# Dilated attention with score terms as half-row matmuls of two heads, q and k recopied per branch, and fewer value loads

## The chip, the cores and the metric

One Trainium2 chip, one core. The time is the device time of one execution of the whole program in microseconds, as the median of several runs. Engines: PE (TensorE), DVE (VectorE), ACT (ScalarE), POOL (GpSimd) and SP (SyncE, which here only issues DMAs).

## What is computed

One step of a hybrid layer for a prompt of 2048 tokens and a few sample tokens: projections to q, k and v, a state-space scan (SSD), a dilated attention of 8 heads of 64, and behind them the trunk (gating, output projection, cross-attention, MLP). The change is in the attention of the prompt. Its three branches have (window, dilation) = (128, 1), (512, 4), (2048, 16); each has blocks of n = 128 queries of one residue, which see the keys of their own block and of the block before:

```python
def dilated_branch_prompt(q, k, v, window, dil):
    n = window // dil
    ...
    qb = to_blocks(q)
    kb = with_prev(to_blocks(k))
    vb = with_prev(to_blocks(v))
    s = jnp.einsum('brjqhd,brjkhd->brjhqk', qb, kb) * (HEAD_DIM ** -0.5)
    ...
    dist = a + n - c
    band = (dist >= 0) & (dist <= n)
    ...
    p, lse = softmax_stats(s)
    o = jnp.einsum('brjhqk,brjkhd->brjqhd', p, vb)
    ...
def combine_branches(outs, lses):
    w = jax.nn.softmax(jnp.stack(lses, axis=0), axis=0)
    return jnp.sum(w[..., None] * jnp.stack(outs, axis=0), axis=0)
```

## The kernel before, in words

The program runs phase_a (projections, 0 to about 300 us), phase_ssd (to about 670), phase_att (about 660 to 1057) and then the trunk. q and k are kept in DRAM as two parts each, a high and a low one (s_qh, s_ql, s_kh, s_kl), since a product in the fast form of fp32 would lose bits: a score is qh·kh + qh·kl + ql·kh. In DRAM the heads lie in 4 groups of two heads, 128 rows (2 x 64) by 2048 tokens.

phase_att works in 96 steps: 4 groups g, 3 branches b, 8 steps each; a step is 2 blocks of 128 queries for both heads (u = 0, 1). In step i the engines get, in this order: front(i), the scores on PE; soft(i), DVE's masked minimum (L995) and ACT's exponential (L997); back(i-2), the values of the step before the last (L1018), after every second step with a copy of the output to SBUF by ACT (L1028); flip(i-1), the transposes of the probabilities (L1005) with their copy to SBUF by DVE (L1010), one in four by ACT (L1008); then the actions that `at` has put down for this step. The first two steps run beside the end of phase_ssd.

The scores of one block (lines 976 to 987): per head one full-row matmul (L983) over 128 rows, where q stands twice, [qh; qh], and k as [kh; kl], and one half-row matmul (L986) over 64 rows for ql·kh. All are 256 keys wide. The keys lie in DRAM permuted within 128 tokens (lines 258 to 269), so that the views of branches 1 and 2 find runs of 8 keys; queries are read with a stride of 4 in branch 1 and of 16 in branch 2.

`load_qk` (lines 923 to 942) loads a group's q and k with 9 DMAs issued by GpSimd into 5 tiles of 1 MB; group g+1 is loaded at step 24g+1, into the other half of a double set of tiles. `load_v` (lines 944 to 959) loads the values with SP: 16 DMAs of 64 KB for branch 0 (L949), 16 for branch 1 (L954), one for branch 2 (L957); the first is called ahead of step 0.

The combine of group g starts at step 24g+24, and its parts follow at +0 (gather, L1053 to L1065: the statistics go to DRAM and come back as t_R), +5 (least, L1069 to L1072), +6 (exponentials, L1075, with products on GpSimd), +7 (coefficients, L1084 to L1094: to DRAM and back as t_cf), and then the products of outputs and coefficients on GpSimd (L1103, L1106), four chunks of 128x512 for three branches. It works in place in the output tiles t_o, of which there are 5. The last group's combine uses DVE too. Step 12 loads columns of gains for the trunk (trunk.weights; DVE scales one, g_gx, at L1435). The trunk's first residual tiles are loaded at steps 73 to 77 and the last three of eight after the last scores, by GpSimd (L1387).

Of the kernel before, what the change touches and what calls it, by code (L numbers as in the profile page):

```python
# [10 lines left out]
F32 = mybir.dt.float32  # L11
# [7 lines left out]
P = 128  # L19
# [8 lines left out]
def host_constants():  # L28
# [10 lines left out]
    off1 = (blk - 1) * P + 16 * (w % 8) + w // 8  # L39
    off2 = (blk - 1) * P + 32 * (w // 32) + 4 * (w % 8) + (w // 8) % 4  # L40
    m1 = np.where((a - off1 >= 0) & (a - off1 <= P), 0.0, BIG)
    m2 = np.where((a - off2 >= 0) & (a - off2 <= P), 0.0, BIG)
# [51 lines left out]
def weight_parts(nc, hi, lo, raw, g):  # L94
    """hi + lo = raw * g exactly to float32."""
    nc.scalar.activation(hi, raw, AF.Copy, scale=g)
    nc.vector.scalar_tensor_tensor(lo, raw, g, hi.bitcast(F32), op0=ALU.mult, op1=ALU.subtract)


def phase_a(E, arena, ssd):  # L100
    """q, k, v, dt of every token; x transposed, in two parts."""
    nc, tc = E.nc, E.tc
    with ExitStack() as ctx, ExitStack() as inner:
# [66 lines left out]
        def memory(j):  # L170
            """The memory's rows, transposed and scaled, in two parts."""
# [33 lines left out]
        def turn(i, b):  # L205
            """Rotary positions; the parts of a block of q | k | v | dt."""
# [29 lines left out]
        def finish(i):  # L236
# [11 lines left out]
            else:  # L248
# [3 lines left out]
                for o, dhi, dlo in ((0, E.s_qh, E.s_ql), (512, E.s_kh, E.s_kl)):  # L252
# [5 lines left out]
                    if o == 0:  # L258
                        nc.scalar.activation(hi, pq, AF.Copy)
                        nc.vector.tensor_tensor(lo, pq, hi.bitcast(F32), op=ALU.subtract)  # L260
                    else:
                        for g in range(4):
                            hv = hi[:, g, :].rearrange("p (r m) -> p m r", r=16)
                            pv = pq[:, g, :].rearrange("p (m r) -> p m r", r=16)
                            nc.scalar.activation(hv, pv, AF.Copy)
                            nc.vector.tensor_tensor(lo[:, g, :].rearrange("p (r m) -> p m r", r=16), pv,
                                                    hv.bitcast(F32), op=ALU.subtract)
# [77 lines left out]
def rstd_rows(E, ps):  # L345
    """The row of 1 / rms of x in DRAM."""
# [6 lines left out]
def softplus(E):  # L353
    """dt of every token and head."""
# [21 lines left out]
def decays(E, sp, psum):  # L376
    """Decay sums and their rows, for every token and head, step by step; psum gives three banks."""
# [44 lines left out]
def phase_ssd(E, arena, early, att):  # L422
    """xBC, conv, SSD; leaves y + D xs transposed, and the sample's conv outputs; step by step as long as
    the phase before it lasts."""
    nc, tc = E.nc, E.tc
    with ExitStack() as ctx:
# [13 lines left out]
        def load(g):  # L440
            """Group g of 256 tokens; the sample's beside the first."""
# [1943 lines left out]
```

## Time and profile before

| | |
|---|---|
| runs | 3629.81 us median of 3 (3623.95 to 3631.62) |
| span of the profiled execution | 3620.6 us, its own time was not recorded beside it |
| granted TensorE clock, mean | 0.969 of full |
| PE busy | 3398.2 us (94%) |
| DVE, ACT, POOL busy | 2024.1 (56%), 1166.9 (32%), 1224.8 (34%) |
| DMA | 451.40 MB, mean 125 GB/s |

The span goes from the first to the last instruction on the core; the time of a run is a little longer. In a row of a timeline stand the start in us, the length in us, the engine, the line, output and inputs by the program's names, shapes and the count of instructions that are drawn together, and in brackets the idle time before it with what ended it. PEld is PE's weight load, SPq and POOLq are the queues of these engines. A matmul's end is modelled, so distances are taken from start to start.

### The profile page before, as it was taken

How to read it: one execution, taken by the hardware profiler on the slowest of the kernel's cores; microseconds unless marked ns; L12 is line 12 of the kernel's file. 1: busy time of each engine (PE TensorE's matmuls, PEld its weight loads, DVE VectorE, ACT ScalarE, POOL GpSimd, SP SyncE). 2: the span in 40 equal slices, each digit the busy share in tenths (PEclk: the TensorE clock that was granted, in tenths of full speed). 3: DMA queues.
4: the chain of work that ended last, by engine and by line, in shares of the span. 5: the costliest groups of instructions: out<-in, count | busy, mean ns of one | idle time of the engine just before them, and what ended most of it. 6: DMA issues, size and time to landing. Idle time of an engine off the chain costs nothing. (4 is left out here: it accounts for less than half of the span.)

```text
span 3620.6 us, 52407 instructions
## 1 busy us (share of the span) xinstructions
PE 3398.2 (94%) x20231; PEld 3005.7 (83%) x20231; DVE 2024.1 (56%) x4116; ACT 1166.9 (32%) x2652; POOL 1224.8 (34%) x1043
## 2 busy tenths in 40 slices
PE   9998988599997999999999999989999999999998
PEld 7998988477776788767777677789988999999998
DVE  5435888456657534467765445555334455555555
ACT  5544333256654333321111111143443311111113
POOL 1114454203433332476641122354223441111113
PEclk9999989699998999999999999999999999999999
DMA  7667342857647322155544533541342222222222
GB/s 207 208 202 209 88 120 69 176 95 143 156 126 200 105 59 59 37 176 195 183 137 151 175 117 97 174 165 41 123 123 65 76 93 93 94 93 93 77 92 95
DMA packets 414043, 451.40 MB, mean 125 GB/s; under 512 B 40892, under 2 KB 347759, under 8 KB 409698
## 3 DMA queue, kind: packets, MB, share of 16 engines
q1 hardware_dynamic: 382914, 382.51, 34.9%
q0 software_dynamic: 30880, 65.54, 7.5%
q8 instruction: 160, 2.62, 0.3%
q14 instruction: 89, 0.73, 0.1%
HBM read 372.52 MB, written 142.44 MB: 142 GB/s over the span
## 5 line engine op out<-in xcount | busy, mean ns | idle before, releaser
L1445 PE MATMUL g_g<-g_b,w_hi 128*128 128x352 f32 (+1 forms) x1760 | 628.0, 358 | 8.3 <-ACT w_hi L1234 8.3
L1446 PE MATMUL g_g<-g_b,w_lo 128*128 128x352 f32 (+1 forms) x1760 | 620.7, 354 | 8.4 <-DVE w_lo L1235 8.4
L1962 POOL TENSOR_TENSOR g_small<-g_small 128x352 f32<-128x352 f32 (+1 forms) x160 | 143.3, 897 | 960.2 <-ACT g_a L1961 960.2
L1235 DVE TENSOR_TENSOR w_lo<-w_raw,w_hi 128x512 fp32r<-128x512 f32 x400 | 353.2, 888 | 191.2 <-ACT w_hi L1234 190.4
L1234 ACT ACTIVATE w_hi<-w_raw 128x512 fp32r<-128x512 f32 x400 | 241.1, 622 | 608.0 <-issue 354.6
L1972 PE MATMUL g_a<-g_a,w_hi 128*128 128x352 f32 (+3 forms) x1076 | 390.9, 363 | 21.6 <-DVE g_a L1982 17.7
L1973 PE MATMUL g_a<-g_a,w_lo 128*128 128x352 f32 (+3 forms) x1076 | 384.9, 358 | 1.3 <-DVE w_lo L1235 1.3
L1974 PE MATMUL g_a<-g_a,w_hi 128*128 128x352 f32 (+3 forms) x1076 | 383.4, 356 | 0.5 <-DVE g_a L1963 0.5
L1445 PEld LDWEIGHTS g_g<-g_b,w_hi 128*128 128x128 f32 x1760 | 334.5, 190 | 54.4 <-ACT w_hi L1234 13.2
L1446 PEld LDWEIGHTS g_g<-g_b,w_lo 128*128 128x128 f32 x1760 | 334.6, 190 | 39.7 <-DVE w_lo L1235 10.0
L1448 PE MATMUL g_g<-g_b,w_hi 128*128 128x352 f32 (+1 forms) x1760 | 367.3, 350 | 0.0
L1982 DVE TENSOR_TENSOR g_a<-g_a,g_a 128x512 f32<-128x512 f32 (+2 forms) x504 | 292.5, 591 | 107.9 <-PE g_a L1974 106.8
L1448 PEld LDWEIGHTS g_g<-g_b,w_hi 128*128 128x128 f32 x1760 | 305.6, 188 | 30.5
L1961 ACT ACTIVATE g_a<-g_small 128x352 fp32r<-128x352 f32 (+1 forms) x160 | 87.9, 551 | 635.1 <-DVE g_small L1960 635.1
L1960 DVE SCALAR_TENSOR_TENSOR g_small<-g_g,g_rb 128x352 f32<-128x352 f32 (+1 forms) x160 | 94.2, 588 | 314.9 <-PE g_g L1448 286.0
L1972 PEld LDWEIGHTS g_a<-g_a,w_hi 128*128 128x128 f32 x1076 | 202.6, 188 | 69.1 <-DVE g_a L1982 29.5
L1445 PE MATMUL g_g<-g_a,w_hi 128*128 128x352 f32 (+1 forms) x632 | 227.3, 361 | 5.1 <-ACT g_a L1514 4.4
L1446 PE MATMUL g_g<-g_a,w_lo 128*128 128x352 f32 (+1 forms) x632 | 225.2, 357 | 3.0 <-DVE w_lo L1235 2.9
L997 ACT ACTIVATE w_spare<-w_spare,t_stats 128x256 f32<-128x256 f32 (+1 forms) x376 | 169.3, 452 | 168.6 <-DVE t_stats L995 168.3
L1974 PEld LDWEIGHTS g_a<-g_a,w_hi 128*128 128x128 f32 x1076 | 203.1, 189 | 23.3 <-DVE g_a L1963 0.9
L1973 PEld LDWEIGHTS g_a<-g_a,w_lo 128*128 128x128 f32 x1076 | 202.7, 188 | 21.7 <-DVE w_lo L1235 1.9
L1963 DVE TENSOR_TENSOR g_a<-g_small,g_a 128x352 fp32r<-128x352 f32 (+1 forms) x160 | 186.4, 1166 | 2.5 <-POOL g_small L1962 2.2
(477 smaller groups left out, 7219.3 us busy)
## 6 DMA issues: line engine op xcount, KB each, us to landing
w_raw<-in_w_up_dram SPq DMA_DIRECT2D x64, 512.0 KB
w_raw<-in_w_down_dram SPq DMA_DIRECT2D x64, 512.0 KB
out_dram<-in_cache_win_k_dram SPq DMA_DIRECT2D x32, 1022.0 KB
out_dram<-in_cache_win_v_dram SPq DMA_DIRECT2D x32, 1022.0 KB
g_wide<-in_cache_win_k_dram SPq DMA_DIRECT2D x32, 512.0 KB
t_cf<-s_coef SPq DMA_DIRECT2D x32, 384.0 KB
g_spare<-in_cache_win_v_dram SPq DMA_DIRECT2D x48, 256.0 KB
a_xn<-in_x_prompt_dram SPq DMA_DIRECT2D x16, 512.0 KB
```

Of the source, the lines that this page charges most:

```text
L997: nc.scalar.activation(pr[:, u, :w], pr[:, u, :w], AF.Exp, bias=nm, scale=-1.0, accum_out=stats[:, 1, u, col:col + 1])
L1234: nc.scalar.activation(hi, src, AF.Copy)
L1235: nc.vector.tensor_tensor(lo, src, hi.bitcast(F32), op=ALU.subtract)
L1445: mm(ps[:, :n], hi[:, k], rhs[0][k][:, s], start=first and k == ks[0], stop=False)
L1446: mm(ps[:, :n], lo[:, k], rhs[0][k][:, s], start=False, stop=False)
L1448: mm(ps[:, :n], hi[:, k], rhs[1][k][:, s], start=False, stop=last and k == ks[-1])
L1962: nc.gpsimd.tensor_tensor(t1[:, :k], t1[:, :k], t1[:, :k], op=ALU.mult)
L1963: line.later(3, lambda: nc.vector.tensor_tensor(ul[:, s], t1[:, :k], uh[:, s].bitcast(F32), op=ALU.subtract))
L1972: mm(ps[:, :k], hi[:, j, c], us[f, j, 0][:, s], start=(j == 0), stop=False)
L1973: mm(ps[:, :k], lo[:, j, c], us[f, j, 0][:, s], start=False, stop=False)
L1974: mm(ps[:, :k], hi[:, j, c], us[f, j, 1][:, s], start=False, stop=(j == 1))
L1982: nc.vector.tensor_tensor(xs[m][:, s], xs[m][:, s], ps[:, :k], op=ALU.add)
```

## The change

Six things change.

1. Scores: per block and head, three half-row matmuls over 64 rows instead of one of 128 and one of 64. The two heads stand on rows 0 to 63 and 64 to 127, and their matmuls alternate. The width is that of the keys needed: 128 in branch 2 and in first blocks, else 256.
2. `load_qk`: the four parts as they lie in DRAM, 4 DMAs and 4 tiles of 1 MB, issued at step 24g+9 instead of 24g+1.
3. New: six copies of 128x2048 on GpSimd a group (`by_residue`), one at each of the steps max(24g, 2) + 0 to 5. They reorder q by residues of 4 (two copies, for branch 1), k by residues of 16 (two, for branches 1 and 2) and q by 16 (two, for branch 2).
4. `load_v`: one DMA instead of 16 for branch 0, four instead of 16 for branch 1.
5. phase_a writes the keys without the permutation, with one ACT and one DVE instruction instead of four each; the masks follow.
6. The trunk's residual tiles 0 to 3 at steps 82 to 85 instead of 0 to 4 at 73 to 77, and four instead of three after the last scores.

```diff
@@ phase_a
-                    if o == 0:
-                        nc.scalar.activation(hi, pq, AF.Copy)
-                        nc.vector.tensor_tensor(lo, pq, hi.bitcast(F32), op=ALU.subtract)
-                    else:
-                        for g in range(4):
...
+                    nc.scalar.activation(hi, pq, AF.Copy)
+                    nc.vector.tensor_tensor(lo, pq, hi.bitcast(F32), op=ALU.subtract)
@@ phase_att
         def load_qk(g):
...
-            for u in range(2):
-                q = st["q", u] = tile()
-                k = st["k", u] = tile()
-                rows = slice(64 * u, 64 * u + 64)
-                nc.gpsimd.dma_start(q[0:64], E.s_qh[g, rows])
-                nc.gpsimd.dma_start(k[rows], E.s_kh[g, rows])
-                nc.gpsimd.dma_start(q[64:128], E.s_qh[g, rows])
-                nc.gpsimd.dma_start(k[64 - 64 * u:128 - 64 * u], E.s_kl[g, rows])
-                if u == 0:
-                    st["l"] = tile()
-                    nc.gpsimd.dma_start(st["l"], E.s_ql[g])
-            return st
+            tiles = []
+            for i, src in enumerate((E.s_qh, E.s_ql, E.s_kh, E.s_kl)):
+                t = trunk.lend(i, T)
+                nc.gpsimd.dma_start(t, src[g])
+                tiles.append(t)
+            return tiles
+
+        def by_residue(tiles, i):
+            src = tiles[(0, 1, 2, 3, 0, 1)[i]]
+            if i < 2:
+                t = trunk.lend(4 + i, T)
+                dst, src = (x.rearrange(y, j=4, r=4) for x, y in ((t, "p (j r i) -> p j i r"), (src, "p (j i r) -> p j i r")))
+            else:
+                t = trunk.lend(4 + i, T) if i < 4 else kp.tile([P, T], F32R, name=f"t_q{i}")
+                dst, src = (x.rearrange(y, r=16) for x, y in ((t, "p (r m) -> p r m"), (src, "p (m r) -> p r m")))
+            nc.gpsimd.tensor_copy(dst, src)
+            return t
 
         def load_v(g, b):
             t = (vp if b else kp).tile([P, 16, P], F32, name="t_v" if b else "t_v0")
             sv = E.s_v[g]
             if b == 0:
-                for r in range(16):
-                    nc.sync.dma_start(t[8 * r:8 * r + 8], sv.rearrange("(j m r) f -> r m j f", r=16, m=8)[r])
+                nc.sync.dma_start(t, sv.rearrange("(j p) f -> p j f", p=P))
             elif b == 1:
...
         def scores(st, b, blk0):
             ps = [pss.tile([P, 2, 256], F32, name=f"t_pss{u}") for u in range(2)]
             for i in range(2):
-                qcols, kview, _, _, _ = where(b, blk0 + i)
-                for u in range(2):
-                    nc.tensor.matmul(ps[u][:, i], st["q", u][:, qcols], kview(st["k", u]), start=True, stop=False)
-                for u in range(2):
-                    half = slice(64 * u, 64 * u + 64)
-                    nc.tensor.matmul(ps[u][:, i], st["l"][half, qcols], kview(st["k", u][half]), start=False, stop=True)
+                qv, kv, vt, _ = where(b, blk0 + i)
+                o = 4 if b == 2 else 0
+                for n, (x, y) in enumerate(((o, 2), (o, 3), (o + 1, 2))):
+                    for u in range(2):
+                        half = slice(64 * u, 64 * u + 64)
+                        nc.tensor.matmul(ps[u][:, i, :P * len(vt)], qv(st[x][half]), kv(st[y][half]),
+                                         start=(n == 0), stop=(n == 2))
             return ps
...
-            ps[i] = scores(st[g], b, blk)
+            ps[i] = scores(st[g] if b == 0 else st16[g], b, blk)
...
-                at(24 * g + 1, lambda g=g: first(g + 1))
+                at(24 * g + 9, lambda g=g: first(g + 1))
...
+            for k in range(6):
+                at(max(24 * g, 2) + k, lambda g=g, k=k: turned(g, k))
...
-        for k in range(5):
-            at(73 + k, lambda k=k: trunk.residual(0, [k]))
+        for k in range(4):
+            at(82 + k, lambda k=k: trunk.residual(0, [k]))
...
-                trunk.residual(0, range(5, 8))
+                trunk.residual(0, range(4, 8))
```

The order of the instructions, at three places. First PE, the end of a step's transposes (t_pt) and the scores of the first of two blocks of the next step in branch 0 (t_pss0 and t_pss1 are the two heads' scores, g_b the tiles of q and k), before:

```order
L1005 MATMUL t_pt_6996<-ident_91,w_spare_6899 128x128 x2
L1005 MATMUL t_pt_7001<-ident_91,w_spare_6899 128x128 x4
L983 MATMUL t_pss0_7022<-g_b1_6748,g_b0_6747 128x256
L983 MATMUL t_pss1_7023<-g_b4_6756,g_b3_6755 128x256
L986 MATMUL t_pss0_7022<-g_b1_6748,g_b2_6753 128x256
L986 MATMUL t_pss1_7023<-g_b4_6756,g_b2_6753 128x256
```

and with the change:

```order
L995 MATMUL t_pt_6875<-ident_91,w_spare_6786 128x128 x2
L995 MATMUL t_pt_6880<-ident_91,w_spare_6786 128x128 x4
L975 MATMUL t_pss0_6887<-g_b2_6655,g_b0_6651 128x256
L975 MATMUL t_pss1_6888<-g_b2_6655,g_b0_6651 128x256
L975 MATMUL t_pss0_6887<-g_b3_6657,g_b0_6651 128x256
L975 MATMUL t_pss1_6888<-g_b3_6657,g_b0_6651 128x256
L975 MATMUL t_pss0_6887<-g_b2_6655,g_b1_6653 128x256
L975 MATMUL t_pss1_6888<-g_b2_6655,g_b1_6653 128x256
```

Four matmuls a block in two forms have become six in one; consecutive ones belong to different heads. The second block of the step follows in the same way.

Second GpSimd's queue, from the loads of group 1's last and group 2's q and k on to the first instruction of the first combine (t_ex), before:

```order
L937 DMA t_qk_7016<-s_qh 64x2048
L938 DMA t_qk_7017<-s_kl 64x2048
L935 DMA g_b_8016<-s_qh 64x2048
L936 DMA g_b_8017<-s_kh 64x2048
L937 DMA g_b_8016<-s_qh 64x2048
L938 DMA g_b_8017<-s_kl 64x2048
L941 DMA g_b_8022<-s_ql 128x2048
L935 DMA g_b_8024<-s_qh 64x2048
L936 DMA g_b_8025<-s_kh 64x2048
L937 DMA g_b_8024<-s_qh 64x2048
L938 DMA g_b_8025<-s_kl 64x2048
L1072 TENSOR_TENSOR t_ex<-t_mn,t_R 32x128 x3
```

and with the change, from the last copies of group 0 over group 1's loads and copies to the same instruction:

```order
L934 COPY t_q_7124<-g_b_6651 128x2048
L934 COPY t_q_7172<-g_b_6653 128x2048
L920 DMA g_b_7262<-s_qh 128x2048
L920 DMA g_b_7264<-s_ql 128x2048
L920 DMA g_b_7266<-s_kh 128x2048
L920 DMA g_b_7268<-s_kl 128x2048
L934 COPY g_b_7915<-g_b_7262 128x4x128x4
L934 COPY g_b_7972<-g_b_7264 128x4x128x4
L934 COPY g_b_8020<-g_b_7266 128x2048
L934 COPY g_b_8069<-g_b_7268 128x2048
L934 COPY t_q_8117<-g_b_7262 128x2048
L934 COPY t_q_8165<-g_b_7264 128x2048
L1062 TENSOR_TENSOR t_ex<-t_mn,t_R 32x128 x3
```

Group 2's loads stood ahead of the combine; now group 1's six copies do, and group 2's loads come behind its small products.

Third SP's queue at the start of the attention (s_v are the values in DRAM, t_v their tile; the first line is the end of phase_ssd), before:

```order
L585 DMA s_y<-s_yg 128x4x256
L1169 DMA t_mask<-in_c_mask_dram 128x640
L949 DMA t_v_6762<-s_v 8x16x128 x16
L639 DMA out_dram<-s_cv 3x1024
L585 DMA s_y<-s_yg 128x4x256
L630 DMA out_dram<-s_fin 128x4x128
L954 DMA t_v<-s_v 8x4x512 x16
L957 DMA t_v<-s_v 128x2048
```

and with the change:

```order
L577 DMA s_y<-s_yg 128x4x256
L1163 DMA t_mask<-in_c_mask_dram 128x640
L941 DMA t_v_6660<-s_v 128x16x128
L631 DMA out_dram<-s_cv 3x1024
L577 DMA s_y<-s_yg 128x4x256
L622 DMA out_dram<-s_fin 128x4x128
L944 DMA t_v<-s_v 32x4x512 x4
L947 DMA t_v<-s_v 128x2048
```

The places in the queue are the same, with 1 and 4 DMAs for 16 and 16.

## Rows read from the trace of the kernel before

**Rows 1.** Waits of PE, 636 to 1140 us: total, times, longest.
```profile
PE t_po L1018 <- DMA t_v<-s_v: 26.0, 1, 26.0
PE t_po L1018 <- DVE t_ptb L1010: 14.6, 3, 6.1
```

**Rows 2.** Busy time by stretch; the first line names the columns.
```profile
core 0: us, PE busy (x) PEld busy (x) DVE busy (x) ACT busy (x) POOL busy (x), PEclk, DMA share, GB/s
...
700.00:720.00 20.00, 16.55 (x144) 13.41 (x145) 10.35 (x38) 8.50 (x30) 0.00 (x0) 0.82 0.58 161
...
840.00:860.00 20.00, 20.00 (x155) 16.51 (x153) 11.38 (x45) 12.69 (x44) 15.55 (x14) 1.00 0.54 114
```

**Rows 3.** Timeline of PE, a step of branch 0: start, length, line, shapes, count.
```profile
899.76 0.49 PE L983 MATMUL t_pss<-g_b,g_b 128*128 128x256 f32 x2
...
900.92 0.38 PE L986 MATMUL t_pss<-g_b,g_b 64*128 64x256 f32 x2
901.24 1.15 PE L1018 MATMUL t_po<-t_ptb,t_v 128*64 128x128 f32 x16
902.31 1.09 PE L1005 MATMUL t_pt<-ident,w_spare 128*128 128x128 f32 x8
903.16 0.48 PE L983 MATMUL t_pss<-g_b,g_b 128*128 128x256 f32 x2
```

**Rows 4.** Timeline of PE, a step of branch 1.
```profile
742.59 0.72 PE L983 MATMUL t_pss<-g_b,g_b 128*128 128x256 f32 x2
...
744.79 1.15 PE L1018 MATMUL t_po<-t_ptb,t_v 128*64 128x128 f32 x16
```

**Rows 5.** Timeline of PE, a step of branch 2.
```profile
861.07 0.48 PE L983 MATMUL t_pss<-g_b,g_b 128*128 128x256 f32 x1
...
863.23 0.66 PE L1018 MATMUL t_po<-t_ptb,t_v 128*64 128x128 f32 x8
...
864.23 0.48 PE L983 MATMUL t_pss<-g_b,g_b 128*128 128x256 f32 x1
```

**Rows 6.** Timeline of PE, a projection with full rows and 256 columns.
```profile
378.08 0.28 PE L480 MATMUL s_psg<-s_x,w_hi 128*128 128x256 f32 x1
378.20 0.28 PE L481 MATMUL s_psg<-s_x,w_lo 128*128 128x256 f32 x1
```

**Rows 7.** Timeline of PE's weight loads, a stream on 32 rows.
```profile
2177.76 0.96 PEld L832 LDWEIGHTS g_s<-g_wide,g_spare 32*128 32x128 f32 x8 [0.37 <-POOL w_raw L1278]
```

**Rows 8.** Timeline of ACT, branch 2: first exponential of a step, output copy.
```profile
866.90 0.40 ACT L997 ACTIVATE w_spare<-w_spare,t_stats 128x128 f32<-128x128 f32 x1 [1.49 <-DVE t_stats L995]
...
868.46 1.01 ACT L1028 ACTIVATE t_o<-t_po 128x512 f32<-128x512 f32 x1
```

**Rows 9.** Timeline of SyncE's queue, issue of the first value tile.
```profile
644.68 52.58 SPq L949 DMA_DIRECT2D t_v<-s_v  x16
```

**Rows 10.** Waits of DVE, 636 to 1140 us.
```profile
DVE t_mn L1069 <- DMA t_R<-s_stat: 13.4, 2, 7.1
...
DVE g_gx L1435 <- DMA g_gx<-in_g_xatt_dram: 6.8, 1, 6.8
```

**Rows 11.** Timeline of SyncE's queue, statistics written and read back.
```profile
794.05 0.34 SPq L1063 DMA_DIRECT2D s_stat<-t_rows  x1
813.66 0.30 SPq L1065 DMA_DIRECT2D t_R<-s_stat  x1
```

**Rows 12.** GpSimd's instructions of two lines: ns min/median/max, first and last start, forms.
```profile
L613 POOL COPY s_xs<-s_xps x1: 374/374/374, 446.6 to 446.6; 128x192 f32<-128x192 f32 x1
...
L1278 POOL TENSOR_TENSOR w_raw<-w_raw,g_gx x16: 1887/1897/2349, 1281.5 to 2657.1; 128x1024 f32<-128x1024 f32 x16
```

**Rows 13.** Timelines of PE, GpSimd and ACT: gather, last sums, next output copy.
```profile
975.65 0.62 PE L1053 MATMUL t_pst<-ident,t_stats 128*48 128x128 f32 x4 [0.56 <-DVE t_ptb L1010]
...
1034.07 2.62 POOL L1106 TENSOR_TENSOR t_o<-t_o 128x512 f32<-128x512 f32 x2
...
1045.21 1.01 ACT L1028 ACTIVATE t_o<-t_po 128x512 f32<-128x512 f32 x1
```

More of the change, by code (lines that the diff above doesn't have):

```diff
@@ L38, in host_constants @@
     blk, w = c // P, c % P
[L39 to L42, printed above, removed]
+    d1 = a - ((blk - 1) * P + w)
+    d2 = a - ((blk - 1) * P + 4 * (w % 32) + w // 32)
+    m1 = np.where((d1 >= 0) & (d1 <= P), 0.0, BIG)
+    m2 = np.where((d2 >= 0) & (d2 <= P), 0.0, BIG)
     m3 = np.where(np.arange(P)[None, :] <= a, 0.0, BIG)
@@ L923, in load_qk @@
         def load_qk(g):
-            st = {}
-            names = iter(range(5) if g % 2 == 0 else range(5, 10))
-            def tile():
-                i = next(names)
-                return kp.tile([P, T], F32R, name=f"t_qk{i}") if i > 7 else trunk.lend(i, T)
-            for u in range(2):
-                q = st["q", u] = tile()
-                k = st["k", u] = tile()
-                rows = slice(64 * u, 64 * u + 64)
-                nc.gpsimd.dma_start(q[0:64], E.s_qh[g, rows])
-                nc.gpsimd.dma_start(k[rows], E.s_kh[g, rows])
-                nc.gpsimd.dma_start(q[64:128], E.s_qh[g, rows])
-                nc.gpsimd.dma_start(k[64 - 64 * u:128 - 64 * u], E.s_kl[g, rows])
-                if u == 0:
-                    st["l"] = tile()
-                    nc.gpsimd.dma_start(st["l"], E.s_ql[g])
-            return st
+            tiles = []
[14 more added lines that the diff above has]
+            return t
         def load_v(g, b):
@@ L947, in load_v @@
             if b == 0:
[L948 to L949 removed]
+                nc.sync.dma_start(t, sv.rearrange("(j p) f -> p j f", p=P))
             elif b == 1:
[L951 to L955 removed]
+                for i in range(4):
+                    nc.sync.dma_start(t[32 * i:32 * i + 32].rearrange("p (c q) f -> p c (q f)", c=4),
+                                      sv.rearrange("(c m s q) f -> s m c (q f)", c=4, m=32, s=4)[i])
             else:
@@ L994, in softmax @@
                 nm = stats[:, 0, u, col:col + 1]
-                nc.vector.tensor_tensor_reduce(out=pr[:, u, :w], in0=ps[u][:, blk % 2, off:off + w], in1=m, scale=1.0,
+                nc.vector.tensor_tensor_reduce(out=pr[:, u, :w], in0=ps[u][:, blk % 2, :w], in1=m, scale=1.0,
                                                scalar=2 * BIG, op0=ALU.add, op1=ALU.min, accum_out=nm)
```

35 lines of the change are left out of this document (13 added, 22 removed).

## The prediction

> **What bounds the kernel now.** The change touches the attention, which runs from about 660 to 1057 us, and little outside it, so I first asked which waits TensorE (PE) has there. Two entries count [rows 1]: one wait of 26.0 us for a value tile, and 14.6 us in three waits for the transposed probabilities. Then I read the busy time by stretches: away from these stalls PE is busy 20.00 us of 20 at full granted clock, ACT 12.69 and DVE 11.38 [rows 2]. So a step there lasts as long as its PE work, and other engines have room. What a step consists of is in the timeline of PE: scores, values, transposes. In branch 0 (window 128) it takes 903.16 - 899.76 = 3.40 us, and the scores, up to the first value matmul, 1.48 of that [rows 3]. In branch 1 the scores take 744.79 - 742.59 = 2.20 [rows 4]. In branch 2 they take 2.16 out of a step of 3.16 [rows 5]. Eight matmuls of the same shapes thus cost 0.7 us more where queries and keys are read with strides. The trunk behind the attention is PE work that does not change, so what the attention saves the kernel saves.
>
> **Scores.** A step now issues four full-row and four half-row matmuls and changes between the forms three times within them. After the change it issues six pairs of half-row matmuls, in one form, with contiguous weights and keys in runs of 32 or longer. No row shows a stream of such pairs. The nearest are a stream of full-row matmuls of 256 columns, 0.12 us from start to start [rows 6], and a stream on 32 rows, where eight weight loads take 0.96 us, so 0.11 each once the last one's own length, some 0.19, is taken off [rows 7]. In both the next weight load is hidden, in the second although all loads go to the same rows. That two matmuls on different parts of the array run side by side is seen in the values: 16 of them, eight pairs, take 1.07 us up to the first transpose [rows 3], 0.86 at 0.107 a pair, and 0.21 for the first load and for leaving the form. So I take 0.12 a pair, 6 x 0.12 = 0.72, add the same 0.21, and 0.17 for entering half rows from the full-row transposes, a change of form that is not there now: 1.10 us, instead of 1.48, 2.20 and 2.16.
>
> Bounds of a pair: below, 0.11 [rows 7]; above, the pair as it stands alone now, 0.32 with its switch (900.92 to 901.24) [rows 3]. I stay near the low end, since a stream in one form is nearer to the other streams than to a lone pair between two forms.
>
> The Trainium skill says, in TensorEngine Tiling (Array Packing), Key Properties, that changing the tiling mode drains TensorE, changing only the tile does not. The rows agree: a switch costs about 0.2 us here. By that rule alone, two switches fewer a step, the gain would be 0.4 x 96 = 38 us; the rest of my term is the strides, which no sentence of that page covers.
>
> Branch 0 then saves 0.38 a step and branch 1 1.10; ACT and DVE still have room in steps of 3.0 [rows 2]. In branch 2 PE would need 2.10 a step, but ACT's four exponentials take 868.46 - 866.90 = 1.56 and every other step an output copy of 1.01 follows [rows 8]; with a flip copy now and then that is 2.1 to 2.2. I take steps of 2.25 there, 0.91 less. Over 32 steps of each branch: 32 x (0.38 + 1.10 + 0.91) = **-77**.
>
> **Value loads.** Sync spent 52.58 us on issuing the 16 DMAs of the first value tile [rows 9], while ten megabytes of q and k for two groups were landing. After the change the tile is one DMA, four megabytes are issued ahead of it, and group 1's come at step 9. So the 26.0 us should go, and the clock loss behind them: the granted clock was 0.82 of full in the 20 us after [rows 2], some 3 us. I leave 3 for a late landing: **-26**. The fewer DMAs of the other value tiles were hidden behind whole branches of 24 us and more: 0.
>
> **The statistics' way.** DVE waits 13.4 us, in two places, for the gathered statistics [rows 10]. In the first, Sync held the DMA that reads them back from 794.05 to 813.66 [rows 11], while the next group's five megabytes of q and k were landing. These loads move to step 9 of the group, away from it. With the lower clock after each wait about 16 us are lost today: **-15**. At step 12 DVE waits 6.8 for a column of gains [rows 10]; group 1's load now falls close to that, so I leave this stall as it is: 0, give or take 7.
>
> **GpSimd's copies.** Six copies of 128x2048 a group are new. The nearest rows are a copy of 128x192 at 374 ns, in proportion 4.0 us for 2048, and products of 128x1024 at 1.90 us, 3.8 for 2048 [rows 12]; half of that is my lower bound, as a copy reads one operand, and twice it the upper one, 7.6, as the copies read or write with strides. I take 4.0. Branch 1 needs four of the six after eight steps, 24 us. The last four overwrite tiles that the group before reads until its last scores, and the combine's subtractions stand behind them in GpSimd's queue; ACT wants these about 18 us into the group, and they need 1.4, which leaves 16.5 for four copies, 4.1 each. At 4.0 nothing is lost; at 7.6 it would be 30.4 - 16.5 = 14 us in each of three groups, 42 in all.
>
> **Buffers of the outputs.** GpSimd's products in the combine free the tiles that ACT writes in branch 2 of the next group. In the third combine they ended at 1034.07 + 2.62 = 1036.7, 61 us after the gather at 975.65, and ACT's copy was there at 1045.21, 8.5 us later [rows 13]. Only the seven steps at the head of that chain get shorter, by 0.4 each: 58 us. ACT's copy comes after 8 x 3.0 + 8 x 3.0 + 3 x 2.25 = 55. So ACT, and PE behind it, will wait 3 us, in three groups, and more where the next load of q and k, now issued just ahead of the products, slows the coefficients down. 5 each: **+15**, between 0 and 40.
>
> The rest is 0: phase A's small copies lie beside a full PE, and the trunk's first tiles (four loaded after the last scores instead of three) come within the same few microseconds, give or take 5.
>
> **Sum.** -77 - 26 - 15 + 15 = -103. The profiled execution's span is 3620.6; the median of the runs, 3629.81, lies 9.2 above it, about what lies around a span. From the median: **3527 us**.
>
> **Rivals.**
> (a) The weight loads are not hidden: the next pair loads into rows that the pair before is using, so load and matmul stand one behind the other, twice 0.11 or 0.22 a pair, and 6 x 0.10 = 0.6 us a step come back. Branch 0 gets slower by 0.2 a step, the other two faster by 0.5: 32 x 0.8 = 26 us instead of 77, and with hardly a wait for buffers 3570. Rows 7 speak against it, one set of rows throughout and no gap. 12%. The Trainium skill has a rule that would do this, in TensorE: Matmul & The Clock Gate, Part 3: a weight load overlaps a running matmul only where the row groups differ.
> (b) Buffers, coefficients and the moved loads cost 35 to 40 instead of 15: 3550. For it: the slack of the output tiles turns negative. Against it: the chain had 8.5 us to spare [rows 13]. 15%.
> (c) The first stall stays, because the value tile is late for another reason than its 16 DMAs: 3553. 5%.
> (d) Slower than before: GpSimd's strided copies are so slow that the combine and branch 1 wait for them. Three groups lose 4c - 16.5 each (branch 1's wait for the copies lies within that) and the first, which has no group before it, 4c - 24. That is 110 us, the gain and the measurement's uncertainty, from about c = 11.5 us a copy, three times the dearest row [rows 12]; at 12 us it gives 3646. 3%, and 2% for copies just short of that.
> (e) The change does not do what it says: a pair costs what a lone pair does, 0.32, in the stream too. The scores would take 2.0 us, branch 0 lose what the others win, and only the stalls go: 3595. 3%.
>
> **Chances.** Mine 60%, the others as given. A measurement of this kernel tells differences above 0.2%, some 7 us. Faster by more: 0.95; within: 0.02; slower: 0.03. The range goes from 3490 (0.11 a pair, no wait for buffers, the gains' stall gone too) to 3580, which takes in (a), (b), (c) and copies of 7 us.
>
> **What would show it.** Steps of 3.0 us in branches 0 and 1 and about 2.25 in branch 2; score pairs 0.12 us apart; no wait for a value tile near 676 us; no wait of DVE for the statistics; copies near 4 us; ACT's output copies waiting for GpSimd in branch 2 of groups 1 to 3. Pairs 0.22 apart would be (a), 0.32 (e); first scores of branch 1 that wait for GpSimd (d). I am wrong altogether if the attention gets shorter by less than 60 us.

## The result and the profile after

The changed kernel takes 3535.83 us (median of 4 runs, 3533.06 to 3540.54); the kernel before, measured with it, 3626.88. The ratio is 0.9747 with a 95% interval of 0.9733 to 0.9761: 91 us less, where 103 were forecast (3527, range 3490 to 3580). The profiled execution has a span of 3531.3 us at a mean granted clock of 0.967.

First the waits between 630 and 1060 us, of PE, ACT, GpSimd and DVE, which answer to [rows 1] and [rows 10] (line, what it waited for, total, times, longest):

```profile
PE t_pt L995 <- ACT w_spare L987: 31.3, 3, 12.9
...
PE t_po L1008 <- DVE t_ptb L1000: 4.7, 7, 3.6
...
ACT t_o L1018 <- POOL t_o L1096: 34.8, 3, 14.0
...
POOL t_o L1093 <- DMA t_cf<-s_coef: 43.6, 3, 17.8
...
DVE g_gx L1431 <- DMA g_gx<-in_g_xatt_dram: 5.0, 1, 5.0
```

The wait for a value tile is gone, that for the transposed probabilities fell from 14.6 to 4.7, and DVE no longer waits for the statistics; the one for the gains' column stands. New is PE's wait for ACT at L995, the transposes: 31.3 us in three places. It starts at ACT, which waits 34.8 us for GpSimd to let go of an output tile (L1018), and GpSimd waits 43.6 us for the coefficients t_cf. GpSimd waited for them in the kernel before too, but in shorter pieces, and ACT did not have to wait behind it:

```profile
POOL t_o L1103 <- DMA t_cf<-s_coef: 38.4, 5, 10.7
```

Now the steps in the timeline of PE (start, length, line). One of branch 0 and one of branch 2, answering to [rows 3, 5]:

```profile
742.56 0.98 PE L975 MATMUL t_pss<-g_b,g_b 64*128 64x256 f32 x12
743.47 1.14 PE L1008 MATMUL t_po<-t_ptb,t_v 128*64 128x128 f32 x16
744.54 1.09 PE L995 MATMUL t_pt<-ident,w_spare 128*128 128x128 f32 x8
745.57 0.98 PE L975 MATMUL t_pss<-g_b,g_b 64*128 64x256 f32 x12
...
862.38 0.88 PE L975 MATMUL t_pss<-g_b,t_q 64*128 64x128 f32 x12
863.19 0.66 PE L1008 MATMUL t_po<-t_ptb,t_v 128*64 128x128 f32 x8
863.78 0.66 PE L995 MATMUL t_pt<-ident,w_spare 128*128 128x128 f32 x4
864.37 0.66 PE L975 MATMUL t_pss<-g_b,t_q 64*128 64x128 f32 x8
```

A step of branch 0 takes 745.57 - 742.56 = 3.01 us with 0.91 for the scores; one of branch 2 takes 864.37 - 862.38 = 1.99 with 0.81. Branch 1 runs at 3.01 too. From the starts of all 96 steps the time of each stage (the 8 steps of one branch in one group) can be summed. Undisturbed stages, and what the disturbed ones take beyond that, in us:

```
                                     before          after     difference   forecast
branch 0, 4 x 8 steps               4 x 26.5       4 x 24.1       - 9.6      \
branch 1                            4 x 31.3       4 x 22.5       -35.2       > -77
branch 2                            4 x 26.7       4 x 17.3       -37.6      /
beyond it: start (group 0, br. 0)     36.8            1.4         -35.4       -26
statistics (groups 1, 2, br. 0)    7.0 + 7.9           0          -14.9       -15
gains' column (group 0, br. 1)         6.7            4.8         - 1.9         0
output tiles (groups 1 to 3, br. 2)    0       16.3+17.1+10.3     +43.7      \ +15
low clock in the steps behind them     0        0.7 + 1.5         + 2.2      /
sum (attention 396.3 -> 307.8)                                    -88.7      -103
```

Without the rounding of the rows the attention is 88.5 us shorter. It also begins 3.1 us earlier and the trunk takes 2.3 longer, which makes the 89.3 of the two spans. The 3.1 are scatter: in the other runs below, all with the same phase A, the attention begins at 658.6 to 662.1 us, here at 657.4 and in the kernel before at 660.5.

The first group with the new loss, group 1, in the timeline of GpSimd, then ACT and PE:

```profile
754.74 0.60 POOL L920 DMA_DIRECT2D g_b<-s_qh  x1
...
756.37 0.57 POOL L920 DMA_DIRECT2D g_b<-s_kl  x1
773.87 3.75 POOL L1093 TENSOR_TENSOR t_o<-t_o,t_cf 128x512 f32<-128x512 f32 x3 [16.94 <-DMA t_cf<-s_coef]
...
796.34 2.60 POOL L1096 TENSOR_TENSOR t_o<-t_o 128x512 f32<-128x512 f32 x2
...
797.64 1.03 ACT L1018 ACTIVATE t_o<-t_po 128x512 f32<-128x512 f32 x1 [13.20 <-POOL t_o L1096]
...
798.98 1.63 PE L995 MATMUL t_pt<-ident,w_spare 128*128 128x128 f32 x4 [12.05 <-ACT w_spare L987]
800.53 1.54 PE L975 MATMUL t_pss<-g_b,t_q 64*128 64x128 f32 x12
```

The loads of the next group are issued from 754.74 to 756.9, ahead of the products; the coefficients, asked for at 756.35, are there for the products 17.5 us later, and these run from 773.87 to 798.9. ACT, which reached its output copy at 784.4, starts it at 797.64, when the first of the last two sums is done. PE comes to a stop for 12 us, and its clock falls: in the stretch after it the granted clock is 0.50, the lower level of 1.2 GHz, and steps take 3.57 instead of 1.99.

The stretches, with the line that names the columns:

```profile
core 0: us, PE busy (x) PEld busy (x) DVE busy (x) ACT busy (x) POOL busy (x), PEclk, DMA share, GB/s
776.00:786.00 10.00, 10.00 (x124) 8.20 (x122) 7.27 (x41) 7.48 (x32) 9.84 (x9) 1.00 0.68 171
786.00:797.00 11.00, 0.93 (x16) 0.61 (x12) 1.03 (x9) 0.00 (x0) 10.92 (x10) 0.62 0.92 199
797.00:807.00 10.00, 8.03 (x50) 5.97 (x51) 3.57 (x20) 7.44 (x31) 9.92 (x5) 0.50 0.22 59
```

In group 3 there is no next group to load, and ACT waits 7.5 us all the same. GpSimd's timeline there, and the first products of the third combine in the kernel before, whose last sums are in [rows 13]:

```profile
928.22 3.75 POOL L1093 TENSOR_TENSOR t_o<-t_o,t_cf 128x512 f32<-128x512 f32 x3 [8.87 <-DMA t_cf<-s_coef]
...
934.52 0.60 POOL L1383 DMA_DIRECT2D g_b<-s_xh  x1
...
954.15 2.60 POOL L1096 TENSOR_TENSOR t_o<-t_o 128x512 f32<-128x512 f32 x2
```

```profile
1011.49 3.76 POOL L1103 TENSOR_TENSOR t_o<-t_o,t_cf 128x512 f32<-128x512 f32 x3 [9.55 <-DMA t_cf<-s_coef]
```

The trunk's residual tiles (point 6 of the change) are now loaded here. Two of their DMAs are issued between each chunk and the next, three times 1.1 us. From the first product to the last sums it takes 25.9 us, against 1034.07 - 1011.49 = 22.6 in the kernel before, where these DMAs came ahead of the combine.

The copies that are new take what was forecast, 3.8 us (ns min/median/max, first and last start):

```profile
L934 POOL CAST g_b<-g_b x16: 3689/3790/3915, 659.3 to 891.6; 128x2048 fp32r<-128x2048 f32 x16
...
L934 POOL CAST t_q<-g_b x8: 3756/3788/3838, 674.3 to 902.7; 128x2048 fp32r<-128x2048 f32 x8
```

### The profile page after: what moved, and what is told of

Its sections match the earlier page's. It is cut to its first block, busy times and chain, and to the rows that moved or that the text cites. A ratio compares the mean times of both kernels' runs of the same rounds, so it can differ in the third digit from the quotient of the medians.

```text
span 3531.3 us, 52948 instructions
## 1 busy us (share of the span) xinstructions
PE 3317.7 (94%) x20615; PEld 2943.7 (83%) x20615; DVE 2009.7 (57%) x4068; ACT 1145.5 (32%) x2604; POOL 1304.9 (37%) x1047
## 3 DMA queue, kind: packets, MB, share of 16 engines
q1 hardware_dynamic: 376066, 382.51, 34.8%
## 5 line engine op out<-in xcount | busy, mean ns | idle before, releaser
L1441 PEld LDWEIGHTS g_g<-g_b,w_hi 128*128 128x128 f32 x1760 | 334.8, 190 | 54.2 <-ACT w_hi L1230 13.2
```

Of the source, the lines that this page charges most:

```text
L1441: mm(ps[:, :n], hi[:, k], rhs[0][k][:, s], start=first and k == ks[0], stop=False)
```

## The experiments

All versions but the last two were run once, and the runs of the changed kernel alone scatter over 7.5 us. So a difference of a few us between two spans decides nothing; the readings rest on steps and waits, which repeat (an undisturbed branch 2 takes 17.3 to 17.4 us in every run with the copies).

**The next load four steps later.** The edit is a number:

```diff
-                at(24 * g + 9, lambda g=g: first(g + 1))
+                at(24 * g + 13, lambda g=g: first(g + 1))
```

> Edit: the next group's q and k are loaded at step 24g+13 instead of 24g+9, nothing else. Theory (the coefficients are slowed by this load, and so GpSimd's products and ACT's output copy): in the changed kernel the coefficients arrive 17.8 and 16.9 us after GpSimd is ready in the groups where the load is issued just ahead of them; here both should fall to about 9, and ACT's waits for the output tiles in branch 2 of groups 1 and 2 (13 and 14 us) to about 6 or 7, that of group 3 (7.4, no load there) stay. With the clock lost behind each wait the span becomes some 15 to 18 us shorter than 3531. Rival (the wait is set by GpSimd's own work, the copies and products): the waits stay at 13 and 14, the span at 3531. The stall at step 14 for the gains' column (5 us) should go too if group 1's load is its cause, and stay if not.

Measured: a time of 3520.62 and a span of 3518.8, 12.5 us less than 3531.3, where 15 to 18 were expected. First GpSimd's timeline at the first product of the first and second combine, with the first DMA of the load between them, then ACT's wait:

```profile
765.01 3.75 POOL L1093 TENSOR_TENSOR t_o<-t_o,t_cf 128x512 f32<-128x512 f32 x3 [9.15 <-DMA t_cf<-s_coef]
...
783.95 0.60 POOL L920 DMA_DIRECT2D g_b<-s_qh  x1
...
841.07 3.76 POOL L1093 TENSOR_TENSOR t_o<-t_o,t_cf 128x512 f32<-128x512 f32 x3 [11.11 <-DMA t_cf<-s_coef]
```

```profile
ACT t_o L1018 <- POOL t_o L1096: 20.9, 3, 7.8
```

In group 1 the coefficients come 9.15 us after GpSimd is ready instead of 16.94, in group 2 after 11.11 instead of 17.82. ACT's waits fall from 34.8 to 20.9 us, the longest from 14.0 to 7.8, and group 3's stage is as long as before (27.9 against 27.6). The branch 2 stages of groups 1 and 2 fall from 33.6 and 34.4 to 26.0 and 27.9. So the load just ahead of the products was about a third of the loss. The rest is not the chain alone: the load's four issues, from 783.95 on, now stand between the third and the fourth chunk and take 2.2 us of GpSimd's time. Without them ACT's wait of 5.6 us in group 1 would be 3.4 (an estimate from these rows). The stall for the gains' column stayed at 7.94, but that part of the run decides nothing: in group 0 the six copies stand ahead of the load in GpSimd's queue until 683, and it was issued at 682.98 as against 681.76. The edit had not moved it there.

**No copies, strided reading.** q and k of a branch are read from the loaded tiles (two sets of four), half-row pairs as in the change:

```diff
-                t = trunk.lend(i, T)
+                t = trunk.lend(i + 4 * (g % 2), T)
...
-                return (lambda t: t[:, P * blk:P * blk + P],
-                        lambda t: t.rearrange("p (s q j m) -> p q j s m", s=4, q=4, j=4)[:, q, j0:j + 1],
+                return (lambda t: t[:, 512 * j + q:512 * j + 512:4],
+                        lambda t: t.rearrange("p (j m s q) -> p q j s m", j=4, m=32, s=4, q=4)[:, q, j0:j + 1],
...
-            return (lambda t: t[:, P * blk:P * blk + P], lambda t: t[:, P * blk:P * blk + P], [blk], 32 + blk)
+            return (lambda t: t[:, blk::16], lambda t: t[:, blk::16], [blk], 32 + blk)
...
-            for k in range(6):
-                at(max(24 * g, 2) + k, lambda g=g, k=k: turned(g, k))
```

> Edit: the six copies are left out; branches 1 and 2 read q and k with strides of 4 and 16 elements straight from the loaded tiles, of which there are two sets; the half-row pairs stay. Theory (about 0.7 us of the gain of a step in branches 1 and 2 comes from contiguous reading, 0.4 from the single form): steps of branch 1 go from 3.01 to 3.5 or more, of branch 2 from 1.99 to 2.6 or more, branch 0 stays at 3.01; some 35 us more PE time in all, partly given back because GpSimd is free and ACT does not wait for output tiles (44 us in the changed kernel). Rival (the strides cost nothing once the form is single): steps stay at 3.01 and 1.99, and the span falls by the output tiles' wait, to about 3490 to 3500.

Measured: span 3540.7. PE's timeline, branch 1 and then branch 2:

```profile
773.08 1.75 PE L975 MATMUL t_pss<-g_b,g_b 64*128 64x256 f32 x12
774.76 1.15 PE L1008 MATMUL t_po<-t_ptb,t_v 128*64 128x128 f32 x16
...
776.86 1.76 PE L975 MATMUL t_pss<-g_b,g_b 64*128 64x256 f32 x12
...
794.94 1.56 PE L975 MATMUL t_pss<-g_b,g_b 64*128 64x128 f32 x12
796.43 0.66 PE L1008 MATMUL t_po<-t_ptb,t_v 128*64 128x128 f32 x8
...
797.60 1.54 PE L975 MATMUL t_pss<-g_b,g_b 64*128 64x128 f32 x12
```

Steps of branch 1 take 3.78 us, the scores 1.68 of it instead of 0.91; of branch 2 2.66, the scores 1.49 instead of 0.81. Branch 0 stays at 3.01. The theory holds with a price of 0.77 and 0.67 us a step, 4 x (28.2 - 22.5) + 4 x (22.7 - 17.3) = 44 us in all, where some 35 were expected. Most of it came back from ACT's waits for output tiles, 10.0 us instead of 34.8, and from the gains' column, which is not waited for here (step 14 takes 3.78), so that the span rose by only 9.4. Against the kernel before, the steps that still read with strides are 0.35 and 0.50 us shorter, and branch 0, where nothing is strided, 0.39: that is what the single form brings, in branches 1 and 2 together with the keys' new layout and in branch 2 with the narrower width.

**Sixteen DMAs for the values of branch 0.**

```diff
-                nc.sync.dma_start(t, sv.rearrange("(j p) f -> p j f", p=P))
+                for r in range(16):
+                    nc.sync.dma_start(t[8 * r:8 * r + 8], sv.rearrange("(j r m) f -> r m j f", r=16, m=8)[r])
```

> Edit: the values of branch 0 are loaded by 16 DMAs of 64 KB again instead of one of 1 MB. Theory of the prediction (the first stall came from these 16 DMAs together with the loads of two groups; four megabytes instead of ten are ahead now): a stall at step 2 of some 3 to 10 us, the span 3531 to 3541. Rival 1 (the number of DMAs alone made the stall): 20 us or more come back, the span is 3550 or more. Rival 2 (only the volume of the loads made it): no stall, span 3531.

Measured: span 3546.6, 15.3 us more, but not where it was looked for. Group 0's branch 0 takes 25.5 us as before this edit: no stall at the start at all. The time went into the step that waits for the gains' column (12.51 instead of 8.15) and into the waits for output tiles (stages of 35.9, 39.4 and 28.8 instead of 33.6, 34.4 and 27.6): the column and the second half of the coefficients stand behind these DMAs in SP's queue. The theory's stall at step 2 did not come: at the start, the number of value DMAs does nothing alone.

**Head by head.**

```diff
-                for n, (x, y) in enumerate(((o, 2), (o, 3), (o + 1, 2))):
-                    for u in range(2):
+                for u in range(2):
+                    for n, (x, y) in enumerate(((o, 2), (o, 3), (o + 1, 2))):
```

> Edit: the three matmuls of one head are issued in a row, then the three of the other, instead of alternating. Theory (the two row halves work side by side only where neighbours in the queue use different halves, 0.11 us a pair): within a head 0.11 us each with at best one overlap at each change of head, so the scores of a step go from 0.92 to about 1.3 us, steps of branches 0 and 1 to about 3.35, branch 2 to 2.3; 30 us more PE time, a part of it hidden in ACT's waits. Rival (each half runs on by itself, whatever the order in the queue): no difference, span 3531.

Measured: span 3535.4, 4.1 more; PE's timeline, a step of branch 1:

```profile
766.22 0.99 PE L975 MATMUL t_pss<-g_b,g_b 64*128 64x256 f32 x12
767.13 1.17 PE L1008 MATMUL t_po<-t_ptb,t_v 128*64 128x128 f32 x16
...
769.26 0.99 PE L975 MATMUL t_pss<-g_b,g_b 64*128 64x256 f32 x12
```

The scores take 0.92 us and the step 3.00: the theory is refuted. The two heads need not alternate in the queue. The 4.1 us are not in the scores: attention is 1.1 longer, the rest lies outside it, and all of it is within the scatter of the runs.

**The loads early again, without copies.** From the kernel without copies:

```diff
-                at(24 * g + 9, lambda g=g: first(g + 1))
+                at(24 * g + 1, lambda g=g: first(g + 1))
```

> Edit: as the kernel without copies (two sets of tiles), and the next group's q and k are loaded at step 24g+1 again, as in the kernel before, beside the gather of the statistics and, for group 1, beside the start. Theory of the prediction (the waits for the statistics at steps 30 and 54 and the first stall come from where these loads stand): against the kernel without copies at step 24g+9, step 31 of 96 (the last of branch 0 in group 1) and step 55 get some 5 to 8 us longer, DVE waits 10 to 15 us for t_R, which it does not now, and step 2 or 3 gets 10 us or more longer, as eight megabytes come at the start instead of four; the span rises from 3541 by 20 to 40, less what ACT's waits for output tiles (11 us) give back. Rival (fewer and simpler DMAs removed both stalls, the place of the load does not matter): step times as at 24g+9, the span within 5 us of 3541.

Measured: span 3526.0, 14.7 us less than with the load at step 9, and no stall in any of the 96 steps. The rival is right on the stalls and a reason of the prediction wrong: with q and k back beside the start and beside the gather, neither the first stall nor the waits for the statistics return. (The rival's span, within 5 us of 3541, was missed, since ACT's waits went too. And for group 1 the edit changed little: without copies ahead of it in GpSimd's queue its load goes out at 661.52 with step 9 in the program and at 660.76 with step 1, so both runs have eight megabytes at the start.) SP's timeline in the changed kernel, and in this one:

```profile
732.47 0.35 SPq L1053 DMA_DIRECT2D s_stat<-t_rows  x1
734.86 0.30 SPq L1055 DMA_DIRECT2D t_R<-s_stat  x1
```

```profile
740.15 0.37 SPq L1053 DMA_DIRECT2D s_stat<-t_rows  x1
748.75 0.30 SPq L1055 DMA_DIRECT2D t_R<-s_stat  x1
```

The way of the statistics, from write to read, takes 2.4 us without a load beside it and 8.6 with it; 19.6 were measured in the kernel before [rows 11], and 8.6 is short enough not to be waited for. ACT does not wait for GpSimd here. So what made the old loads so harmful was something else than their place, and three runs looked for it.

**Value DMAs in number and size as before, loads of q and k in pieces of 64 rows as before, and both**, each from the kernel with the early loads:

```diff
-                nc.sync.dma_start(t, sv.rearrange("(j p) f -> p j f", p=P))
+                for r in range(16):
+                    nc.sync.dma_start(t[8 * r:8 * r + 8], sv.rearrange("(j r m) f -> r m j f", r=16, m=8)[r])
...
-                nc.gpsimd.dma_start(t, src[g])
+                for u in range(2):
+                    nc.gpsimd.dma_start(t[64 * u:64 * u + 64], src[g, 64 * u:64 * u + 64])
```

(the first run has the first hunk, and likewise 16 DMAs for branch 1; the second run the second hunk; the third all.)

> Edit: as the kernel without copies whose loads of q and k stand at step 24g+1 (span 3526.0, no stall), with 16 DMAs of 64 KB for the values of branch 0 and 16 for branch 1 again. Theory now (the first stall needs many small value DMAs on SP's queue and large loads on GpSimd's queue at the same time): step 2 gets 15 us or more longer than 2.8, PE waits for a value tile, the span is 3545 or more; the statistics' way stays as it is (8.6 us from write to read), since no value DMA is queued there. Rival (the form of q's and k's loads alone made the stall): step 2 stays near 2.8, the span within 10 us of 3526.

> Edit: as the kernel without copies and with loads at step 24g+1, but each tile of q and k is loaded by two DMAs of 64 rows (512 KB) instead of one of 128 rows. Theory (DMAs of 64 rows, as the kernel before had them, hold up the small transfers of the statistics): the read of the statistics is issued 15 us or more after the write instead of 8.6, DVE waits 5 us or more for t_R at steps 31 and 55, the span rises by 10 to 20 from 3526. Rival (the load's volume, five megabytes instead of four, or the place of other DMAs made these waits): the read stays at 8 to 10 us behind the write, no wait of DVE for t_R, span within 5 us of 3526.

> Edit: both, 16 value DMAs and q and k loaded by DMAs of 64 rows. If the stalls of the kernel before have separate causes, the value DMAs for the first and the 64-row loads for the statistics, both are back here and the span is the sum of the two single changes, 3560 or more. If the first stall needs both together, only here step 2 gets 20 us or more longer. If neither is the cause, step 2 and steps 31 and 55 stay as they are without stall.

Measured, spans: 3539.4 with 16 value DMAs, 3540.6 with loads of 64 rows, 3572.1 with both, against 3526.0. SP's timeline with 16 value DMAs, at the start:

```profile
642.86 16.43 SPq L942 DMA_DIRECT2D t_v<-s_v  x16
```

with loads of 64 rows, at the start and at the first gather, and DVE's wait for the statistics:

```profile
642.60 0.79 SPq L942 DMA_DIRECT2D t_v<-s_v  x1
...
740.53 0.35 SPq L1054 DMA_DIRECT2D s_stat<-t_rows  x1
757.41 0.30 SPq L1056 DMA_DIRECT2D t_R<-s_stat  x1
```

```profile
DVE t_mn L1060 <- DMA t_R<-s_stat: 9.9, 2, 5.0
```

and with both, at the start, and PE's wait for the value tile:

```profile
644.32 38.65 SPq L943 DMA_DIRECT2D t_v<-s_v  x16
```

```profile
PE t_po L1011 <- DMA t_v<-s_v: 21.1, 1, 21.1
```

With 16 value DMAs alone SP needs 16.43 us to issue them, and step 2 keeps its 2.79; the loss is again the gains' column, a step of 11.49 instead of 3.78. With the loads in eight DMAs of 64 rows alone the value tile, one DMA, is issued in 0.79 and step 2 takes 2.94, but the statistics need 16.9 us from write to read, DVE waits 9.9 us for them, and the last steps of branch 0 in groups 1 and 2 take 9.62 and 9.56 instead of 3.00. With both, SP needs 38.65 us for the 16 DMAs, PE waits 21.1 for the tile and step 2 takes 25.49. The two stalls are told apart: the statistics wait because the loads of q and k come in pieces of 64 rows, the first value tile only where such loads and 16 small DMAs meet. The pieces bring back 13.1 of the 14.9 us of the statistics, both together 23.8 of the 35.4 at the start. Whether it is the rows of a DMA or the double number of DMAs that counts was not tried, and these runs are without the copies: the two edits were not undone in the changed kernel itself.

**An earlier combine.** From the kernel with the load at step 13:

```diff
-            times = (0, 4, 4, 4, 6, 6, 7, 7) if g == 3 else (0, 5, 6, 7, 10, 11, 12, 14, 17, 17, 17, 17)
+            times = (0, 4, 4, 4, 6, 6, 7, 7) if g == 3 else (0, 3, 4, 5, 8, 9, 10, 14, 17, 17, 17, 17)
...
-                at(max(24 * g, 2) + k, lambda g=g, k=k: turned(g, k))
+                at(max(24 * g, 2) + k + (2 if g and k > 3 else 0), lambda g=g, k=k: turned(g, k))
```

> Edit: as the kernel with the load at 24g+13, and the combine's parts come at steps +3, +4, +5 and +8, +9, +10, +14 instead of +5, +6, +7 and +10, +11, +12, +14; GpSimd's two copies for branch 2 (t_q) go from +4, +5 to +6, +7 behind the combine's small products, in groups 1 to 3. Theory (the output copy waits because GpSimd's products end 6 to 8 us too late, and they are late since the coefficients' way starts late, not because they are long): the products start about 6 us earlier, ACT's three waits of 6 to 8 us for the output tiles shrink to 0 to 2, the lost clock behind them too, and the span falls by some 20 to 28, from 3519 to 3491 to 3499. Rival (the products and copies fill GpSimd so that starting earlier shifts nothing): the waits stay, the span stays near 3519. A price could be a wait of DVE for t_R at +3, up to 2 us in three groups.

Measured: span 3510.3, 8.5 less, not 20 to 28. The waits of ACT and of PE:

```profile
ACT t_o L1018 <- POOL t_o L1096: 2.1, 1, 2.1
...
PE t_pss L975 <- DMA g_b<-s_kl: 8.3, 2, 4.5
```

The output tiles cost 2.1 us now instead of 20.9, so the theory is right on what set them: the products only had to begin sooner. What is left is in group 3, where the trunk's DMAs stand between the products. But a new wait took nearly half of the gain: the first steps of groups 2 and 3 take 9.43 and 8.77 us instead of 4.81 and 3.91, since the load of their q and k, which GpSimd issues behind the third chunk, arrives too late. With these faster stages the load at step 13 has no room.

**The gains' column on GpSimd**, from this kernel:

```diff
-        nc.vector.tensor_scalar(self.gx, self.gx, -1.0 / 16, None, op0=ALU.mult)
+        nc.gpsimd.tensor_scalar(self.gx, self.gx, -1.0 / 16, None, op0=ALU.mult)
```

> Edit: as the kernel with the early combine, and the column of gains that trunk.weights loads at step 12 is scaled by GpSimd instead of DVE. Theory (the 8 us step at step 14 is DVE standing in its queue before a load whose way takes 4 to 5 us, whatever the other loads do): that step falls from 7.9 to 3.0, and the span by 5 against the kernel with the early combine. Rival (PE waits there for something else): no change.

Measured: 3507.02 us, ratio to the kernel before 0.9664 (0.9647 to 0.9681); span 3504.8, 5.5 less. The step falls from 7.99 to 3.01: it was DVE that stood before the column. The theory's "whatever the other loads do" is another matter. In GpSimd's queue the scaling stands ahead of the load of group 1, which so went out only at 698.04. SP issued the first three columns from 690.06 to 694.58 here, and from 688.65 to 698.17 in the changed kernel, where that load is issued from 681.76 on. The 5 us between the two are as much as DVE waited, so by these rows the load beside the columns made that wait; no run moved the load alone. In the kernel before it was not this load, which had gone out by 675, but 16 value DMAs ahead of the columns in SP's queue, as in the runs above that have them.

**The load between the chunks**, from this one, step 24g+10 instead of 24g+13:

> Edit: as the kernel with the early combine and the gains on GpSimd (3507.0), the next group's q and k at step 24g+10, so between GpSimd's second and third chunk instead of behind the third. Theory (the first steps of groups 2 and 3 are 6 us too long each because the load comes 4 to 5 us too late for their scores): these two steps fall from 9.5 and 9.0 to about 3.5; the coefficients of the last chunk may come later, up to 5 us, and ACT's copy in branch 2 wait 0 to 4 for it. The time falls by 4 to 12, to 3495 to 3503. Rival (the wait only moves to the output tiles): no change within 2.

Measured: 3504.89 us, ratio 0.9666 (0.9650 to 0.9682): no difference that the intervals could show, where 4 to 12 us were expected. Group 3's first step fell to 3.89, group 2's stayed at 9.20, and a step of branch 2 ahead of it rose to 4.53. GpSimd's timeline:

```profile
770.42 0.62 POOL L920 DMA_DIRECT2D g_b<-s_qh  x1
...
798.62 3.69 POOL L934 CAST g_b<-g_b 128x2048 fp32r<-128x2048 f32 x1 [1.03 <-DMA g_b<-s_kl]
```

Issued at 770.42, the last of the four tiles has landed only at 798.62, 28 us for 4 MB. The values of the next group and the stores of the combine were under way beside it; which of them held it up was not followed. These two are the fastest versions of this study, 29 to 31 us below the change by their medians; their ratios' intervals lie below the change's.

## Why the prediction was right, point by point

- **Scores**, -77: -82.4 by the step sums. The pair at 0.12 was right: read one by one in the step at 742.56, the two matmuls of a pair start within 0.004 us and the pairs 0.11 to 0.12 apart, the first two 0.22. The scores take 0.91 in branch 0 where 1.10 less the part that lies in the transposes, 0.93, was worked out, and the step 3.01 where 3.02 was. The 0.7 us for the strides is shown by the run without copies: 0.77 and 0.67. Branch 2 was undersized: I let ACT set a step of 2.25, and it takes 1.99, with ACT's exponentials and output copies just fitting.
- **Rival (a)**, unhidden loads, is out: each half gets six matmuls a step on the same rows, and they take 0.91 together. The rule of the Trainium skill named there (TensorE: Matmul & The Clock Gate, Part 3) would have made it 0.22 a pair; the measurement decides against it, as [rows 7] did. That the heads alternate plays no role either.
- **First stall**, -26: -35.4; the clock behind the stall and the slowed steps beside phase_ssd were worth more than the 3 us I put for them. The place was right and the cause half right: 16 DMAs and the form of the loads together. Eight megabytes at that time made no stall by themselves; ten were not tried. That the loads of group 1 were moved was not needed either (early loads: no stall).
- **Statistics**, -15: -14.9, right in size, wrong in cause. I wrote that the loads "move to step 9 of the group, away from it". The move was not needed: with 128 rows in one DMA there is no wait without it. Whether the move alone would have done, with 64 rows, was not tried.
- **GpSimd's copies**, 0: 3.8 us each, no wait for them in the changed kernel. Rival (d) is out.
- **Output tiles**, +15 (0 to 40): +46, beyond its own range. The mechanism, its place and its three groups were as put; the size was the failed term. Rival (b), given 15%, was this mechanism at 35 to 40, and even that was passed. I had 58 us for the chain against 55 for ACT, and "5 each". Measured are 13.2, 14.0 and 7.5 of waiting. The chain without any load would be about 3 to 4 us late, as worked out: 3.4 by the run with the later load (above), and in group 3 the 7.5 less the 3.4 that the trunk's DMAs take between the products, 4.1 (estimates from these traces). Three sizes were wrong. The load just ahead of the products, for which "5 each" leaves 2, cost some 10 in groups 1 and 2. The trunk's tiles, which I put among the zeros, cost those 3.4 in group 3. And the some 3 us of low clock behind each wait were not in the term. So the move of q's and k's load that I credited with a gain was a loss, and the trunk's a smaller one.
- **Gains' column**, 0: -1.9. It stands, and costs 5, for another reason than before (see the run with the gains on GpSimd).
- **Start of the sum**: the 9.2 us between span and median are not "about what lies around a span". A run's time lies 1.8 us above its span here (3533.06 against 3531.3); the rest was scatter between runs. The forecast starts from the median and does not suffer from it.

The first stall gave 9 us more than forecast, the scores 5 and the column 2, and the output tiles took 31 more; so the total, -91 against -103, is nearer than its parts. That is luck: what the first stall gave has nothing to do with what the output tiles took.

## What to carry to other kernels

When a change shortens the steps that an asynchronous chain was hidden behind, work out the chain's end against its reader again for each stage, and count the lost clock behind a stall with the stall. The order of the queue decides what a moved load hits: what stands ahead of it (six copies) can keep it where it was, what is asked for right behind it comes later (the coefficients, though SP asks for them), and the issues themselves take the time of the engine that has other work to do (GpSimd's products). And a stall that goes away with three edits at once has not been explained until the edits are undone one by one and in pairs.

## What the runs showed of the hardware

- Reading q and k with strides of 4 and 16 elements cost nearly as much again as the matmuls themselves: six pairs with contiguous operands 0.91 us, with strides 1.68 (256 columns); with 128 columns 0.81 and 1.49. Which of the two operands costs it was not separated.
- Two matmuls on the two row halves overlapped whatever their order in the queue: twelve of them took 0.91 us alternating and 0.92 head by head, under 0.08 each, where full-row matmuls of this width follow each other in 0.12 [rows 6].
- The same 4 MB in eight DMAs of 64 rows instead of four of 128 doubled the way of small transfers on another queue (16.9 against 8.6 us) and, beside 16 value DMAs, made their issue last 38.65 us instead of 16.43.
- Each DMA that GpSimd issued took 0.5 to 0.6 us of its queue: two between each chunk of products and the next made them 25.9 us long instead of 22.6.
- A wait of 12 us in PE was followed by a stretch at a granted clock of 0.50, and steps of 3.57 instead of 1.99.
